# Second product of an MLP: order of emission on three engines, residual rows requested in three places, mixer weights in two rows

## Chip, cores and metric

The kernel runs on one core of one Trainium2 chip. The metric is the device time of one execution in microseconds, taken as the median of several runs.

## What is computed

A trunk of two layers over 1024 positions of width 1024, all in float32. Each layer has a token mixer (a gated MLP over chunks in the first layer, differential attention in the second), a squared-ReLU MLP of width 4096, and a per-layer gate:

```python
for i in range(DEPTH):
    a = _rmsnorm(h, g_mix_pre[i])
    m = _chunked_gmlp(a, ...) if i % N_MIXERS == 0 else _diff_attention(a, ...)
    h = h + _rmsnorm(m, g_mix_post[i])
    f = _sqrelu_mlp(_rmsnorm(h, g_ffn_pre[i]), f_w_up[i], f_w_down[i])
    h = h + _rmsnorm(f, g_ffn_post[i])
    gate = jax.nn.sigmoid(_rmsnorm(h, g_ple_pre[i]) @ ple_w_gate[i] + ple_b_gate[i])
    e = gate * (p[i] @ ple_w_proj[i])
    h = h + _rmsnorm(e, g_ple_post[i])

def _sqrelu_mlp(x, w_up, w_down):
    return jnp.square(jax.nn.relu(x @ w_up)) @ w_down
```

## The kernel before

Every operand of a product is cut into a high and a low part: ScalarE rounds it into `hi`, VectorE subtracts (`lo`), and TensorE makes three matmuls of 128x512 columns for each pair (`mm3`, L351 to L354). Both products of the MLP are done by a seven-product scheme on 2x2 blocks, so that sums and differences of blocks are formed on VectorE before and after.

**The second product** (in `ffn`, from L697). It has 56 steps `(g, c)`: groups g = 0, 1 and 2 have 16 steps each, group g = 3 has 8. A step is 24 matmuls: four places p, two halves e, three matmuls each. The text calls g = 0 to 3 the first to the fourth group. Around step m stand three jobs:

- `load_down(n)` requests the operands of step n on SP's queue: the activations `hid`, the weight blocks of `f_w_down`, and in the third and fourth group the stored sums `t4`. The operands go to one of seven rooms, the weights to buffers x from a ring (`sets`).
- `split_down(n)` forms the sums of weight blocks (L740 to L755) and cuts them (`cut`, L522 to L524). In the second and third group it also stores a sum to `t4`.
- `evict(g, p)` (L781 to L796) takes the banks of a place to the rows of `MA` when a group ends. TensorE cannot start the next group in a bank before it is evicted.

`after(t)`, called behind step t, emits the splits of step t + 2 or t + 3 (`lead_s`) and then the loads of step t + 7 (`lead_l`; fewer at the end).

The order of emission is not the order of execution. TensorE keeps it over the whole program (`manual_schedule` for PE); on the other engines a planner places the instructions at build time, by its own estimate of when each is ready, earlier emitted ones first among the ready ones.

**The rows behind it.** When the third group ends, `half` and `whole` finish rows of tiles 0 to 3 of the eight row tiles; those of 4 to 7 follow at the end of the fourth group. `whole` calls `residual` (L332), which takes the next of two buffers `hin`, requests the row tile of the residual stream (L336), adds (L340), stores it (L342), and lets `pre_norm` (L328 to L330) normalise it into a row of `MA`. `transpose_to` emits the eight transposes of each tile (L296) and their cuts (L282, L283) at a due time counted in matmul columns. The banks of the transposes are two, `PT`.

**Weights for the next stages** come through `WStream`: `load` requests a weight row into a buffer `raws` (L88) and cuts it into a slot (L119, L120). In the fourth group `ws.load()` is called for the gate's weights; `resident` loads four more operands, cut by ScalarE and GpSimd (L113, L114). `ple`, the gate, begins with a request of the bias row into `bbc` on GpSimd's queue (L847) and adds it at L862. `mixer1`, the second layer's mixer, takes its first weights through `[raw] + hin`.

Of the kernel before, what the change touches and what calls it, by code (L numbers as in the profile page):

```python
# [18 lines left out]
P = 128  # L19
D = 1024  # L20
T = 1024
NT = T // P
# [109 lines left out]
def _trunk(ctx, tc, nc, a, out):  # L132
# [197 lines left out]
        nc.scalar.activation(x, h, AF.Copy, scale=s)  # L330
        transpose_to(x, tt, us, gain)

    def residual(tt, t_ap, rs, hsrc, hdst, pre, gain=None):

        h = hinR.next()
        nc.sync.dma_start(h, hsrc[tt * P:(tt + 1) * P, :])  # L336
        w = D if pre or tt < NT - 1 else 512
        for c in range(0, D, w):
            cs = slice(c, c + w)
            nc.vector.scalar_tensor_tensor(out=h[:, cs], in0=t_ap[:, cs], scalar=rs, in1=h[:, cs],  # L340
                                           op0=ALU.mult, op1=ALU.add)
            nc.sync.dma_start(hdst[tt * P:(tt + 1) * P, cs], h[:, cs])  # L342
        if pre:
            pre_norm(h, tt, pre, gain)
# [170 lines left out]
    def ffn(i, hsrc, hdst, next_weights):  # L515
# [133 lines left out]
        def stream():  # L649
            for q in range(NQ):  # L650
                if q < 3:
                    settle((4, 6, 7)[q])
                yield from load_up(q)

        LEAD = 6
        loads = stream()
        early = [(q, n) for qs in ((0, 1), (2,), (3,), (4,)) for n in (1, 2) for q in qs]
        stage = [x.rearrange("p (r k f) -> p r k f", r=2, f=P) for x in (raw, bbc, raw, bbc, bbc)]
# [37 lines left out]
        def cols(x, k):  # L696
            return x[:, k * 512:k * 512 + 512]  # L697
# [1 line left out]
        sets = [  # L699
            Ring([(MA[:, 1], cols(MA[:, 2], 0)), (MA[:, 3], cols(MA[:, 2], 1)), (raw, cols(MA[:, 4], 0)),  # L700
                  (MA[:, 5], cols(MA[:, 4], 1)), (MA[:, 6], cols(bbc, 0))]),
            Ring([(x, cols(MA[:, t], 1)) for t, x in zip((0, 7, 2, 3, 4), hin + [xn[0], raw, bbc])]),
            Ring([(x, cols(MA[:, t], 1)) for t, x in zip((6, 5, 4, 7), [hin[1], raw, bbc, hin[0]])]),
        ]


        sumR = Ring([cols(xn[1], k) for k in range(2)])
        steps = [(g, c) for g in range(4) for c in range(NQ if g < 3 else NQ // 2)]
        loaded, cuts, ssq = {}, {}, {}

        def load_down(n):
            g, c = steps[n]
            room = last[c] if g == 3 else rooms[n % 7]
            hi, lo = [f32r(x.rearrange("p k t -> p (k t)")) for x in room]
            wh, hh, wl, hl = hi[:, 0:1024], hi[:, 1024:], lo[:, 0:1024], lo[:, 1024:]
            x = sets[g].next() if g < 3 else None
            if g == 3:
                for k in range(2):
                    nc.sync.dma_start(f32(cols(hl, k)), hid[2 * c + k][:, 3072:])
                nc.sync.dma_start(f32(wl), t4[c])  # L720
            else:
                if g == 2:
                    for k in range(2):
                        nc.sync.dma_start(cols(x[0], k), down[c, k, 1])
                    nc.sync.dma_start(x[1], cols(t4[c // 2], c % 2))
                else:
                    nc.sync.dma_start(x[0], down_rows[c, 0])
                    nc.sync.dma_start(x[1], down[c, 1, 1 - g])
                nc.sync.dma_start(f32(hl), hid[c][:, g * 1024:g * 1024 + 1024])
            loaded[n] = wh, wl, hh, hl, x  # L730

        def split_down(n):
            g, c = steps[n]
            wh, wl, hh, hl, x = loaded.pop(n)
            if g < 3:
                a1, a2 = cols(x[0], 0), cols(x[0], 1)
            if g == 0:

                t = sumR.next()
                vec(out=t, in0=a2, in1=a1, op=sub)  # L740
                vec(out=a2, in0=x[1], in1=t, op=sub)
                w = x[0],
            elif g == 1:

                t = sumR.next()
                vec(out=t, in0=a2, in1=a1, op=sub)
                vec(out=a1, in0=x[1], in1=a1, op=sub)
                nc.sync.dma_start(cols(t4[c // 2], c % 2), a1)
                w = x[1], t
            elif g == 2:  # L750

                t = sumR.next()
                vec(out=t, in0=a2, in1=a1, op=sub)
                vec(out=x[1], in0=x[1], in1=t, op=sub)
                nc.sync.dma_start(cols(t4[c // 2], c % 2), x[1])  # L755
                w = t, a2
            else:
                w = f32(wl),
            cut(hh, hl, f32(hl))
            k = D // len(w)  # L760
            for j, v in enumerate(w):
                cut(wh[:, j * k:j * k + k], wl[:, j * k:j * k + k], v)
            cuts[n] = wh, wl, hh, hl

        def after(t):

            for n in range(len(steps)):
                if n - t == lead_s[n]:
                    split_down(n)
            for n in range(len(steps)):  # L770
                if n - t == lead_l[n]:
                    load_down(n)

        for k, n in enumerate(rest_of):
            next(loads, None)
# [28 lines left out]
        def whole(tt, us):  # L804
            s = ssq[tt]
            vec(out=s[:, 0:1], in0=s[:, 0:1], in1=s[:, 1:2], op=add)
            rstd_of(s[:, 0:1], D, RMS_EPS)
            residual(tt, MA[:, tt, :], s[:, 0:1], hsrc, hdst, us)

        for m, (g, c) in enumerate(steps):  # L810
            wh, wl, hh, hl = cuts.pop(m)
            n_c = NQ if g < 3 else NQ // 2

            for p in range(4):
                for e in range(2):
                    bank = PM[p] if e == 0 or g == 3 else other[p]
                    cw = slice(e * 512, e * 512 + 512)
                    ch = slice(e * 512 + p * P, e * 512 + p * P + P)
                    mm3(bank, hh[:, ch], hl[:, ch], wh[:, cw], wl[:, cw],
                        c == 0 and (g < 3 or e == 0), c == n_c - 1 and (g < 3 or e == 1))  # L820
                if c == n_c - 1:
                    evict(g, p)
                    if g == 3:
                        half(p + 4, 0)
                        whole(p + 4, US_F + 4.0 * p)
            if g == 1 and c == 4:
                load_gbc(2 + i)
            if g == 2 and 2 <= c < 6:
                half(c - 2, 0)
            if c == n_c - 1 and g == 2:  # L830
                for p in range(4):
                    half(p, 1)
                    whole(p, US_F + 7 + 4.0 * p)
                for p in range(4):
                    half(p + 4, 1)
                next_weights(i)
            after(m)
            if g == 3:
                if c < 4:
                    ws.load()  # L840
                elif c < 6:
                    res[i] += [resident(i, 2 * c - 8), resident(i, 2 * c - 7)]
# [315 lines left out]
    def mixer1(gi, hsrc, hdst):  # L1158
# [3 lines left out]
        nc.gpsimd.dma_start(sgc, a["subln"])  # L1162
        nc.vector.tensor_scalar(out=sgc, in0=sgc, scalar1=1.0 - LAMBDA_INIT, scalar2=None, op0=ALU.mult)
        pbR.i = 2 * (pmR.i % 3)
        ws.raws = Ring([raw] + hin)
        for cb in range(2):
            qkv_qk(cb, qD, HD ** -0.5, cosT, sinT)
# [267 lines left out]
```

## Time and profile before

| | |
|---|---|
| time, median of 3 runs | 2401.24 us (2396.24 to 2403.47) |
| profiled execution | 2402.34 us, span 2400.6 us |
| TensorE matmul | 2327.9 us, 97%, 10748 instructions |
| VectorE | 1609.3 us, 67% |
| ScalarE | 1165.4 us, 49% |
| GpSimd | 228.0 us, 9% |
| granted TensorE clock, mean | 0.989 |

The span runs from the first to the last instruction of the profiled execution. A busy share is an average over stages with different limits, so stages are read by themselves. In the rows below PE is TensorE, PEld its weight loads, DVE VectorE, ACT ScalarE, POOL GpSimd and SP the queue that issues nearly all transfers; `out<-in` names the buffers, and what stands in brackets is idle time of the engine before the instruction and what ended it. L numbers are lines of the kernel before.

### The profile page before, as it was taken

Reading aid. Unit: us, or ns where it says so; the run is one execution under the profiler, and the core shown is the slowest. Engines: PE = TensorE matmul, PEld = TensorE weight load, DVE = VectorE, ACT = ScalarE, POOL = GpSimd, SP = SyncE. Lnnn points to the kernel's source line nnn. Section 1 sums busy time; section 2 is a strip of 40 time slices with the busy share of each in tenths; the row PEclk is TensorE's granted clock in tenths of the full one; section 3 lists DMA queues with packets and bytes.
Section 4 is the critical chain, followed back from the end, with each engine's and each line's share of the span. In section 5 each row is a group of like instructions: output and inputs, shape, how many; then the busy total and the mean of one; then the engine's idle time right before and its main releaser. Section 6 shows DMA issues by size and latency. Waiting matters only on the chain. (4 is left out here: it accounts for less than half of the span.)

```text
span 2400.6 us, 30544 instructions
## 1 busy us (share of the span) xinstructions
PE 2327.9 (97%) x10748; PEld 1924.2 (80%) x10748; DVE 1609.3 (67%) x2492; ACT 1165.4 (49%) x2003; POOL 228.0 (9%) x303
## 2 busy tenths in 40 slices
PE   9999999999999899999999989999999999989998
PEld 7888888888788687878887878777888888868787
DVE  4733697777866765563335888868877797675654
ACT  6232575555433355462224666657555554334551
POOL 1100100000000022010001342321000000000310
PEclk9999999999999999999999999999999999999999
DMA  9111545446977765244445765554544588777423
GB/s 330 57 35 54 165 142 202 145 156 223 355 249 236 250 233 183 74 169 142 147 154 179 218 181 143 158 184 137 189 159 164 173 335 279 243 256 245 176 106 123
DMA packets 200425, 441.03 MB, mean 184 GB/s; under 512 B 21040, under 2 KB 55856, under 8 KB 200144
## 3 DMA queue, kind: packets, MB, share of 16 engines
q1 hardware_dynamic: 199840, 437.89, 54.4%
q8 instruction: 85, 1.39, 0.2%
q0 software_dynamic: 432, 1.19, 0.2%
q14 instruction: 68, 0.56, 0.1%
HBM read 310.02 MB, written 133.17 MB: 185 GB/s over the span
## 5 line engine op out<-in xcount | busy, mean ns | idle before, releaser
L364 PE MATMUL pm_a<-w,xh 128*128 128x512 f32 x704 | 223.9, 396 | 1.3 <-ACT w L119 0.9
L364 PEld LDWEIGHTS pm_a<-w,xh 128*128 128x128 f32 x704 | 131.6, 189 | 29.8 <-ACT w L119 2.6
L523 ACT ACTIVATE xh<-xl 128x1024 fp32r<-128x1024 f32 x72 | 75.4, 1055 | 148.9 <-DMA xl<-hid 137.5
L364 PE MATMUL pb<-w,xh 128*128 128x512 f32 x416 | 134.9, 400 | 5.5 <-DVE gbc L972 2.9
L524 DVE TENSOR_TENSOR xl<-xl,xh 128x1024 fp32r<-128x1024 f32 x72 | 87.4, 1221 | 78.6 <-ACT xh L523 75.6
L364 PE MATMUL pm_a<-w,xl 128*128 128x512 f32 x352 | 138.7, 394 | 0.0
L523 ACT ACTIVATE w<-ma 128x512 fp32r<-128x512 f32 x130 | 82.2, 634 | 115.6 <-PE pm_a L353 39.5
L524 DVE TENSOR_TENSOR s<-s 128x1024 fp32r<-128x1024 f32 x56 | 68.0, 1222 | 58.9 <-ACT s L523 58.9
L523 ACT ACTIVATE s<-s 128x1024 fp32r<-128x1024 f32 x56 | 58.5, 1054 | 97.6 <-DMA s<-hid 80.6
L847 POOL DMA_DIRECT2D bbc<-in_ple_b_gate_dram x2 | 1.3, 628 | 1077.1 <-DVE s L524 1077.1
L353 PE MATMUL pm_a<-xl,w 128*128 128x512 f32 x260 | 101.4, 390 | 0.2 <-DVE xl L283 0.2
L352 PE MATMUL pm_a<-xh,w 128*128 128x512 f32 x260 | 101.6, 391 | 0.0
L354 PE MATMUL pm_a<-xh,w 128*128 128x512 f32 x260 | 101.2, 389 | 0.0
L364 PEld LDWEIGHTS pb<-w,xh 128*128 128x128 f32 x416 | 77.1, 190 | 20.1 <-DVE xn L394 3.4
L524 DVE TENSOR_TENSOR w<-ma,w 128x512 fp32r<-128x512 f32 x130 | 88.6, 683 | 0.7 <-ACT w L523 0.7
L243 POOL TENSOR_SCALAR small<-small 128x1 f32<-128x1 f32 x104 | 34.7, 333 | 553.9 <-DVE small L397 322.0
L340 DVE SCALAR_TENSOR_TENSOR hin<-ma,small,hin 128x1024 f32<-128x1024 f32 (+1 forms) x49 | 61.6, 1260 | 37.0 <-DMA hin<-h 24.5
L364 PE MATMUL pb<-w,xl 128*128 128x512 f32 x208 | 82.9, 399 | 0.0
L352 PE MATMUL pb<-xh,w 128*128 128x512 f32 x204 | 79.7, 391 | 0.0
L354 PE MATMUL pb<-xh,w 128*128 128x512 f32 x204 | 79.4, 389 | 0.0
L353 PE MATMUL pb<-xl,w 128*128 128x512 f32 x204 | 79.4, 389 | 0.0
L364 PEld LDWEIGHTS pm_a<-w,xl 128*128 128x128 f32 x352 | 66.4, 189 | 12.9
(476 smaller groups left out, 7048.2 us busy)
## 6 DMA issues: line engine op xcount, KB each, us to landing
xl<-hid SPq DMA_DIRECT2D x56, 512.0 KB, 5.1
ma<-in_f_w_up_dram SPq DMA_DIRECT2D x48, 512.0 KB, 3.7
h<-hin SPq DMA_DIRECT2D x40, 512.0 KB, 3.1
hid<-ma SPq DMA_DIRECT2D x80, 256.0 KB, 2.4
s<-hid SPq DMA_DIRECT2D x40, 512.0 KB, 5.2
hin<-h SPq DMA_DIRECT2D x40, 512.0 KB, 3.5
hid<-xn SPq DMA_DIRECT2D x64, 256.0 KB, 2.6
hid<-hin SPq DMA_DIRECT2D x64, 256.0 KB, 2.7
```

The lines of the kernel that those rows point to most:

```text
L243: nc.gpsimd.tensor_scalar(out=ss, in0=ss, scalar1=1.0 / n, scalar2=eps, op0=ALU.mult, op1=ALU.add)
L340: nc.vector.scalar_tensor_tensor(out=h[:, cs], in0=t_ap[:, cs], scalar=rs, in1=h[:, cs], op0=ALU.mult, op1=ALU.add)
L352: nc.tensor.matmul(ps, lhsT=lh, rhs=rh, start=start, stop=False)
L353: nc.tensor.matmul(ps, lhsT=lh, rhs=rl, start=False, stop=False)
L354: nc.tensor.matmul(ps, lhsT=ll, rhs=rh, start=False, stop=stop)
L364: nc.tensor.matmul(ps, lhsT=xs(l, kc, tt * P), rhs=r[:, cs], start=kc == 0 and k == 0, stop=kc == KC - 1 and k == 2)
L523: act(h, v, AF.Copy)
L524: vec(out=l, in0=v, in1=f32(h), op=sub)
L847: nc.gpsimd.dma_start(bbc, a["ple_b_gate"][i:i + 1, :].broadcast_to([P, D]))
```

## The change

- The steps of the first three groups up to step 44 (`FREE` = 45) are emitted inside a second `manual_schedule` that also covers SP, ScalarE and VectorE, so that these engines keep the order of emission there. `after` is rearranged: from step 9 on the loads come first, then the stores of `t4` collected from the split before, then the splits.
- The buffers of the second and third group are three rings of halves (`thirds`). The second group requests its weights as three pieces of 256 KB; the third takes `t4` into its own operand room.
- `residual` can be given its row. Rows are requested by `fetch` into `hin` and `bbc` in turn: 0 and 1 behind step 11 of the third group, 2 behind step 14, 3 to 6 at that group's end, and 7 in the fourth group's end.
- `mixer1` loads its next two weights through rows 2 and 3 of `MA` before it goes on with `[raw] + hin`.

```diff
--- before.py
+++ after.py
@@ -330,10 +330,14 @@
         nc.scalar.activation(x, h, AF.Copy, scale=s)
         transpose_to(x, tt, us, gain)
 
-    def residual(tt, t_ap, rs, hsrc, hdst, pre, gain=None):
-
-        h = hinR.next()
+    def load_h(h, tt, hsrc):
         nc.sync.dma_start(h, hsrc[tt * P:(tt + 1) * P, :])
+        return h
+
+    def residual(tt, t_ap, rs, hsrc, hdst, pre, gain=None, h=None):
+
+        if h is None:
+            h = load_h(hinR.next(), tt, hsrc)
         w = D if pre or tt < NT - 1 else 512
         for c in range(0, D, w):
             cs = slice(c, c + w)
@@ -653,6 +657,7 @@
                 yield from load_up(q)
 
         LEAD = 6
+        FREE = 3 * NQ - 3
         loads = stream()
         early = [(q, n) for qs in ((0, 1), (2,), (3,), (4,)) for n in (1, 2) for q in qs]
         stage = [x.rearrange("p (r k f) -> p r k f", r=2, f=P) for x in (raw, bbc, raw, bbc, bbc)]
@@ -699,21 +704,30 @@
         sets = [
             Ring([(MA[:, 1], cols(MA[:, 2], 0)), (MA[:, 3], cols(MA[:, 2], 1)), (raw, cols(MA[:, 4], 0)),
                   (MA[:, 5], cols(MA[:, 4], 1)), (MA[:, 6], cols(bbc, 0))]),
-            Ring([(x, cols(MA[:, t], 1)) for t, x in zip((0, 7, 2, 3, 4), hin + [xn[0], raw, bbc])]),
-            Ring([(x, cols(MA[:, t], 1)) for t, x in zip((6, 5, 4, 7), [hin[1], raw, bbc, hin[0]])]),
         ]
+
+
+        h0, h1, rw, bb, x0 = [[cols(x, k) for k in range(2)] for x in (*hin, raw, bbc, xn[0])]
+        ma = [cols(MA[:, t], 1) for t in range(NT)]
+        thirds = {
+            1: ([h0[0], h1[0], x0[0], rw[0], bb[0], ma[3], ma[2], ma[1]],
+                [x0[1], h0[1], h1[1], rw[1], ma[5]],
+                [ma[0], ma[7], bb[1], ma[4], ma[6]]),
+            2: ([ma[7], rw[0], h0[0], h1[0], bb[1], ma[4], bb[0]],
+                [h0[1], h1[1], rw[1], ma[5], ma[6]] * 3 + [x0[1]]),
+        }
 
 
         sumR = Ring([cols(xn[1], k) for k in range(2)])
         steps = [(g, c) for g in range(4) for c in range(NQ if g < 3 else NQ // 2)]
-        loaded, cuts, ssq = {}, {}, {}
+        loaded, cuts, ssq, stores = {}, {}, {}, []
 
         def load_down(n):
             g, c = steps[n]
             room = last[c] if g == 3 else rooms[n % 7]
             hi, lo = [f32r(x.rearrange("p k t -> p (k t)")) for x in room]
             wh, hh, wl, hl = hi[:, 0:1024], hi[:, 1024:], lo[:, 0:1024], lo[:, 1024:]
-            x = sets[g].next() if g < 3 else None
+            x = sets[0].next() if g == 0 else [r[c % len(r)] for r in thirds.get(g, ())]
             if g == 3:
                 for k in range(2):
                     nc.sync.dma_start(f32(cols(hl, k)), hid[2 * c + k][:, 3072:])
@@ -721,19 +735,24 @@
             else:
                 if g == 2:
                     for k in range(2):
-                        nc.sync.dma_start(cols(x[0], k), down[c, k, 1])
-                    nc.sync.dma_start(x[1], cols(t4[c // 2], c % 2))
+                        nc.sync.dma_start(x[k], down[c, k, 1])
+                elif g == 1:
+                    for k in range(2):
+                        nc.sync.dma_start(x[k], down[c, 0, k])
+                    nc.sync.dma_start(x[2], down[c, 1, 0])
                 else:
                     nc.sync.dma_start(x[0], down_rows[c, 0])
-                    nc.sync.dma_start(x[1], down[c, 1, 1 - g])
+                    nc.sync.dma_start(x[1], down[c, 1, 1])
                 nc.sync.dma_start(f32(hl), hid[c][:, g * 1024:g * 1024 + 1024])
+                if g == 2:
+                    nc.sync.dma_start(f32(cols(wl, 0)), cols(t4[c // 2], c % 2))
             loaded[n] = wh, wl, hh, hl, x
 
         def split_down(n):
             g, c = steps[n]
             wh, wl, hh, hl, x = loaded.pop(n)
             if g < 3:
-                a1, a2 = cols(x[0], 0), cols(x[0], 1)
+                a1, a2 = x[:2] if g else (cols(x[0], 0), cols(x[0], 1))
             if g == 0:
 
                 t = sumR.next()
@@ -744,15 +763,13 @@
 
                 t = sumR.next()
                 vec(out=t, in0=a2, in1=a1, op=sub)
-                vec(out=a1, in0=x[1], in1=a1, op=sub)
-                nc.sync.dma_start(cols(t4[c // 2], c % 2), a1)
-                w = x[1], t
+                vec(out=a1, in0=x[2], in1=a1, op=sub)
+                w = x[2], t
             elif g == 2:
 
                 t = sumR.next()
                 vec(out=t, in0=a2, in1=a1, op=sub)
-                vec(out=x[1], in0=x[1], in1=t, op=sub)
-                nc.sync.dma_start(cols(t4[c // 2], c % 2), x[1])
+                vec(out=a1, in0=f32(cols(wl, 0)), in1=t, op=sub)
                 w = t, a2
             else:
                 w = f32(wl),
@@ -760,16 +777,31 @@
             k = D // len(w)
             for j, v in enumerate(w):
                 cut(wh[:, j * k:j * k + k], wl[:, j * k:j * k + k], v)
+            if g in thirds:
+                stores.append((cols(t4[c // 2], c % 2), a1))
             cuts[n] = wh, wl, hh, hl
 
         def after(t):
 
+            def begin():
+                for n in range(len(steps)):
+                    if n - t == lead_l[n]:
+                        load_down(n)
+
+            def store():
+                while stores:
+                    nc.sync.dma_start(*stores.pop(0))
+
+            if t + 7 >= NQ:
+                begin()
+                store()
             for n in range(len(steps)):
                 if n - t == lead_s[n]:
                     split_down(n)
-            for n in range(len(steps)):
-                if n - t == lead_l[n]:
-                    load_down(n)
+            if t + 7 < NQ:
+                begin()
+            if t >= FREE:
+                store()
 
         for k, n in enumerate(rest_of):
             next(loads, None)
@@ -805,9 +837,23 @@
             s = ssq[tt]
             vec(out=s[:, 0:1], in0=s[:, 0:1], in1=s[:, 1:2], op=add)
             rstd_of(s[:, 0:1], D, RMS_EPS)
-            residual(tt, MA[:, tt, :], s[:, 0:1], hsrc, hdst, us)
-
+            residual(tt, MA[:, tt, :], s[:, 0:1], hsrc, hdst, us, h=rows.pop(tt))
+
+
+        rows, rowR = {}, Ring(hin + [bbc])
+
+        def fetch(*tts):
+            for tt in tts:
+                rows[tt] = load_h(rowR.next(), tt, hsrc)
+
+
+
+        E = mybir.EngineType
+        strict = tc.manual_schedule(engines={E.PE, E.SP, E.Activation, E.DVE})
+        strict.__enter__()
         for m, (g, c) in enumerate(steps):
+            if m == FREE:
+                strict.__exit__(None, None, None)
             wh, wl, hh, hl = cuts.pop(m)
             n_c = NQ if g < 3 else NQ // 2
 
@@ -823,6 +869,8 @@
                     if g == 3:
                         half(p + 4, 0)
                         whole(p + 4, US_F + 4.0 * p)
+                        if p == 0:
+                            fetch(7)
             if g == 1 and c == 4:
                 load_gbc(2 + i)
             if g == 2 and 2 <= c < 6:
@@ -831,10 +879,17 @@
                 for p in range(4):
                     half(p, 1)
                     whole(p, US_F + 7 + 4.0 * p)
+                    if p == 0:
+                        fetch(3)
+                fetch(4, 5, 6)
                 for p in range(4):
                     half(p + 4, 1)
                 next_weights(i)
             after(m)
+            if g == 2 and c == NQ - 5:
+                fetch(0, 1)
+            if g == 2 and c == NQ - 2:
+                fetch(2)
             if g == 3:
                 if c < 4:
                     ws.load()
@@ -1162,6 +1217,11 @@
         nc.gpsimd.dma_start(sgc, a["subln"])
         nc.vector.tensor_scalar(out=sgc, in0=sgc, scalar1=1.0 - LAMBDA_INIT, scalar2=None, op0=ALU.mult)
         pbR.i = 2 * (pmR.i % 3)
+
+        ws.raws = Ring([MA[:, 2, :], MA[:, 3, :]])
+        settle(3)
+        for _ in range(2):
+            ws.load()
         ws.raws = Ring([raw] + hin)
         for cb in range(2):
             qkv_qk(cb, qD, HD ** -0.5, cosT, sinT)
```

## The prediction

> **What bounds the kernel now.** I read the head of the page first, then the list of TensorE's waits, then the granted clock in short stretches, then the time lines around the longest waits.
>
> ```profile
> span 2400.6 us, 30544 instructions
> PE 2327.9 (97%) x10748; PEld 1924.2 (80%) x10748; DVE 1609.3 (67%) x2492; ACT 1165.4 (49%) x2003; POOL 228.0 (9%) x303
> ```
>
> TensorE is the bound, so only its idle time and its slow time can be won. All its idle time is 2400.6 - 2327.9 = 72.7 us. The list of waits says where the touched stages (second product, the rows behind it, the start of the mixer) hold some of it; columns are total us, times, longest.
>
> ```profile
> PE pt L296 <- DVE xl L283: 8.9, 3, 4.1
> PE pm_c L352 <- DVE ma L789: 8.3, 2, 8.1
> PE pm_a L352 <- DVE ma L789: 7.6, 1, 7.6
> PE pm_a L352 <- ACT s L119: 4.5, 1, 4.5
> ...
> PE pm_a L352 <- DVE hin L601: 2.3, 1, 2.3
> ...
> PE pm_a L352 <- DVE ma L794: 1.2, 1, 1.2
> PE pm_c L352 <- DVE ma L794: 1.2, 1, 1.2
> ...
> PE pt L352 <- DVE ma L787: 0.4, 1, 0.4
> ```
>
> A wait also costs after it ends. The stretches behind the waits (columns: window, length, busy time of each engine, then granted clock, DMA share, GB/s), with an undisturbed one first:
>
> ```profile
> 560.00:600.00 40.00, 40.00 (x179) 33.10 (x178) 31.96 (x48) 23.00 (x33) 0.00 (x0) 1.00 0.69 244
> 792.40:800.00 7.60, 7.45 (x18) 5.13 (x18) 7.60 (x13) 3.99 (x9) 0.00 (x0) 0.58 0.79 283
> 913.80:918.50 4.70, 4.70 (x18) 3.90 (x19) 1.92 (x3) 2.77 (x4) 3.56 (x2) 0.64 0.96 328
> 1065.00:1069.00 4.00, 4.00 (x11) 3.10 (x12) 1.38 (x2) 3.06 (x5) 0.74 (x2) 0.57 0.66 233
> 2135.00:2142.00 7.00, 6.63 (x17) 4.59 (x18) 7.00 (x11) 4.15 (x9) 0.00 (x0) 0.63 0.80 272
> 2256.30:2261.00 4.70, 4.63 (x18) 3.98 (x19) 2.00 (x4) 2.85 (x4) 3.62 (x2) 0.64 0.99 355
> ```
>
> Length times (1 - clock) is what each stall costs again: 7.60 x 0.42 = 3.2, 7.00 x 0.37 = 2.6, 4.70 x 0.36 = 1.7 twice, 4.00 x 0.43 = 1.7 us.
>
> **Part 1, order of emission on SP, ScalarE and VectorE (both layers).** The longest waits stand between the second and the third group. VectorE and ScalarE there, in the first layer:
>
> ```profile
> 788.80 1.06 ACT L523 ACTIVATE s<-s 128x1024 fp32r<-128x1024 f32 x1 [3.87 <-DMA s<-hid]
> 789.89 1.23 DVE L524 TENSOR_TENSOR s<-s 128x1024 fp32r<-128x1024 f32 x1 [2.21 <-ACT s L523]
> 791.63 0.68 DVE L789 TENSOR_TENSOR ma<-pm_a,ma 128x512 f32<-128x512 f32 x1
> 792.46 0.76 PE L352 MATMUL pm_a<-s 128*128 128x512 f32 x1 [7.57 <-DVE ma L789]
> ```
>
> L789 is the first eviction of the group; TensorE cannot start the next group before it. It stands on VectorE behind the cut of a step several steps ahead, and that cut waited for ScalarE, which waited for a transfer of hid. In the order of emission the evictions of the last step come before the cuts that are written after it, so L789 runs as soon as its bank is complete, three quarters of a step (4 us, below) before TensorE wants it. Its work is short (0.68 us), and what is late next is small: where the first and second group meet, the eviction (L787) is in time but for the 0.4 us at the foot of the list. Gain: 7.6 + 8.1 idle and 3.2 + 2.6 clock = 21.5 us.
>
> In the Trainium skill, "TensorE: Matmul & The Clock Gate", section "Part 1: The HAM clock gate", the clock halves after an idle window of about 3.4 us and returns after about 3.4 us of work. By that page one stall costs 1.7 us more, the two boundaries 3.4 instead of 5.8, and the sum would end 2.4 us higher; the trace, with stretches at 0.58 and 0.63 over 7 us and more, disagrees in the size, and I keep the rows.
>
> What the strict order can cost: an instruction that waits now holds all behind it on its engine for the 45 steps of groups one to three. Per step VectorE has two differences, one wide and two half cuts, 4 x 0.68 + 1.23 = 3.95 us, and TensorE 24 matmuls:
>
> ```profile
> 701.00:784.00 83.00, 83.00 (x366) 68.70 (x367) 52.34 (x71) 28.52 (x42) 0.00 (x0) 1.00 0.74 244
> 883.00:906.00 23.00, 21.75 (x101) 17.72 (x99) 19.50 (x26) 14.76 (x27) 13.77 (x15) 1.00 0.45 160
> ```
>
> 83.00 / 366 x 24 = 5.4 us. VectorE is 63% busy there, ScalarE 34%. Loads go out seven steps (38 us) and cuts three steps (16 us; two in the first group) ahead, and a load waits in SP's queue only for the end of a matmul step or a cut emitted before it. The stores of t4 now stand behind the next step's loads, at most one step later; their buffers come round after five to eight steps. I cover all that by the lead and cost it at nothing; without that cover each 0.1 us per step is 9 us over both layers. The new rings and the t4 row that lands in the step's own operand room move no bytes; the second group loads three times 256 KB where it loaded 512 and 256, one more issue per step, 32 in all, on a queue with room. Zero.
>
> The start of the second product waits on L601, 2.3 us: evictions of the first product. They are emitted outside the ordered stretch, so nothing new keeps cuts that are ready from going ahead of them. Between 2.3 us won and as much lost in each layer; I take 0, since the first two cuts and all of L601 stay outside.
>
> **Part 2, residual rows fetched in three places (both layers).** In the fourth group:
>
> ```profile
> 898.09 7.05 SPq L336 DMA_DIRECT2D hin<-h  x2
> 903.65 1.15 ACT L330 ACTIVATE ma<-hin,small 128x1024 f32<-128x1024 f32 x1 [1.42 <-POOL small L244]
> 909.12 1.29 DVE L340 SCALAR_TENSOR_TENSOR hin<-ma,small,hin 128x1024 f32<-128x1024 f32 x1 [5.31 <-DMA hin<-h]
> 910.44 1.06 ACT L328 ACTIVATE ma<-hin 128x1024 f32<-128x1024 f32 x1 [2.50 <-DVE hin L340]
> 912.44 1.06 ACT L282 ACTIVATE xh<-pt 128x512 fp32r<-128x512 f32 x2
> 913.79 0.66 PE L296 MATMUL pt<-identr,ma 128*128 128x128 f32 x4 [4.12 <-DVE xl L283]
> ```
>
> The two requests at 898.09 and just before 905.14 are the third and fourth row. The fourth waits for the second row's buffer, which L330 reads until 904.80. Its late landing stops L340, then ScalarE's L328, and behind that L282, which should have emptied the transposes' bank. With bbc as a third buffer the third row is there before the group ends and the fourth takes the first row's buffer, the one that the request at 898.09 got, 6.7 us before 904.80. L340 moves forward by about as much, L282 is next in line when its transposes end, and TensorE's wait goes. Late next is the transposes' own cut, 0.6 + 0.7 us, beside matmuls. Gain: 4.12 and its twin of 4.1 in the second layer, and twice 1.7 of clock: 11.7 us. Between 0 (ScalarE's order stays bad) and 11.7; I take 11.7, as the chain of six rows starts at the request that moves.
>
> bbc also takes the gate's bias row (L847, on GpSimd's queue), which now waits for the sixth row:
>
> ```profile
> DMA to landing us min/median/max: 5.4/5.6/5.7
> ...
> 947.02 1.14 ACT L330 ACTIVATE ma<-hin,small 128x1024 f32<-128x1024 f32 x1
> 961.13 0.71 PE L364 MATMUL pm_a<-w,xh 128*128 128x512 f32 x2
> ```
>
> The sixth row is read until 948.2; plus 5.6 the bias lands at 953.8. TensorE needs the first pair of banks back at 961.13 (fourth row tile), so 7 us are spare. Queued behind: GpSimd's roots of rows seven and eight, VectorE's later work behind L862. Cost 0; each us beyond the spare costs one, twice.
>
> **Part 3, gate weights pushed back, mixer weights in two rows.** The first four gate weights are cut today inside the third group (836 to 882 us, first layer):
>
> ```profile
> L120 DVE SCALAR_TENSOR_TENSOR w<-raw,gcol,w 128x512 fp32r<-128x512 f32 x8 | 5.7, 749 | 5.8 <-ACT w L119 5.8
> ```
>
> raw is in the ring until the group's last step now, so these eight (5.7 us of VectorE) fall into the stretch 883 to 906, where VectorE is 19.50 of 23 us busy. Bounds: 2.4 us won (the L794 waits) to 2 x 5.7 = 11.4 us lost. Cuts for the matmuls are emitted earlier than these and two of the residual rows no longer wait, so I stay near the low end: 1 us a layer, 2 us lost.
>
> The mixer, second layer only:
>
> ```profile
> 1059.87 0.33 SPq L88 DMA_DIRECT2D hin<-in_w_qkv_dram  x1
> 1064.21 1.33 ACT L119 ACTIVATE s<-hin,gcol 128x512 fp32r<-128x512 f32 x2 [1.28 <-DMA hin<-in_w_qkv_dram]
> ```
>
> The fourth weight goes out when a residual row lets hin go. In a row of MA, whose transposes the first product waits for anyway, it can go out before and land before 1060. Gain 4.5 (the fourth entry of the waits) + 1.7 = 6.2 us; at worst 0, as the buffer comes from rows that are read no more.
>
> **Sum.** The profiled execution took 2402.34 us (span 2400.6), 1.1 above the median 2401.24. 2402.3 - 21.5 - 11.7 - 6.2 + 2.0 = 2364.9, against the median 2363.8: **2364 us**.
>
> **Rivals.** *Only the boundaries come.* ScalarE's order between L328 and L282 is not fixed in the fourth group, which lies behind the ordered stretch, and the mixer's hoist is free too. Without both 2401.2 - 21.5 = 2379.7, with the mixer 2373.5: 2377 between them. *Crowding on VectorE.* The gate cuts land whole on the path, +9.4 over my 2: 2373. For it speaks this pair, where a sum of 128x1 takes 2.36 us beside GpSimd, longer than a cut of 128x1024 (1.23):
>
> ```profile
> 882.22 5.22 POOL L114 TENSOR_TENSOR s<-s 128x1024 fp32r<-128x1024 f32 x2 [33.16 <-ACT s L113]
> 885.09 2.36 DVE L806 TENSOR_TENSOR small<-small 128x1 f32<-128x1 f32 x1
> ```
>
> Four such holds a layer cost 2 x 4 x 2.36 = 18.9 us at most, 2383. The Trainium skill, "SBUF — State Buffer", section "Who interferes with whom", has that lock: a VectorE instruction with two SBUF inputs and a GpSimd one that reads block each other whole; the trace agrees with 2.36 us here. *The order does not bring the eviction forward*, or another wait stands there: 2401. *Slower:* one mechanism, head-of-line waiting in the strict stretch, a load on SP or a cut on VectorE that every step must sit out. It eats the gain at 37.4 / 90 = 0.42 us a step and shows as slower from 0.50; at 0.6 the time is 2364 + 54 = 2418. Against it stand 37% free VectorE and the leads above.
>
> **Numbers.** Forecast 0.49 (2354 to 2371), boundaries only 0.23, crowding 0.12, no effect 0.07, slower 0.09. The low end takes in the start of the product in both layers, L794 and no crowding (2364 - 4.6 - 2.4 - 2.0 = 2355, and up to 3 us, an estimate from the sizes above, for the clock behind the first of these); the high end boundaries only with part of the crowding, 2389. 0.3% is 7.2 us, about what can be told here: faster 0.84, same 0.07, slower 0.09.
>
> **What would show it.** Right: no L789 entry above 1 us among TensorE's waits; the clock at 1.00 behind the second group; L340 without a 5 us wait on hin, L283 gone as TensorE's releaser in the fourth group; L119 gone at the mixer's start; the first L862 later against the end of the fourth group by some 10 us. Wrong: TensorE waits on L524 in steps of groups one to three, new waits on L794 or L524 around 883, or on L862.

## Result and profile after

The changed kernel takes 2374.78 us (median of 4 runs, 2373.36 to 2375.9) where the kernel before takes 2402.35: a ratio of 0.9882, 95% interval 0.9869 to 0.9895. The forecast was 2364 us, the range 2352 to 2389. The median of before has one run more than in the table above. So the sign and the range held: 28 us came where 38 were forecast. The time lies above the forecast's own band (2354 to 2371) and next to the rival "only the boundaries come", which gave 2373.5 with the mixer's wait gone; and the parts differ more than the sum.

Line numbers from here on are those of the changed kernel: the eviction at the end of the second group is L821 (L789 before), that of the third L826 (L794), the residual's request L334, its addition L344, the first product's additions L605, the cuts of the second product L527 and L528.

The head of the page after:

```profile
span 2371.7 us, 30563 instructions
PE 2316.4 (98%) x10748; PEld 1919.4 (81%) x10748; DVE 1603.4 (68%) x2492; ACT 1167.3 (49%) x2003; POOL 235.7 (10%) x303
```

TensorE's idle time fell from 72.7 to 2371.7 - 2316.4 = 55.3 us, and its busy time by 11.5 us with the same 10748 matmuls, while the mean granted clock rose from 0.989 to 0.994. The list of TensorE's waits after (total us, times, longest), the rows of the touched stages:

```profile
PE pt L296 <- DVE xl L283: 7.3, 4, 3.9
PE pt L296 <- ACT ma L330: 4.4, 2, 2.2
...
PE pm_c L356 <- DVE ma L826: 3.9, 3, 1.9
...
PE pm_a L356 <- DVE ma L826: 2.2, 2, 1.6
...
PE pm_a L356 <- DVE hin L605: 0.6, 1, 0.6
```

L821 is not in the list, and neither is L119 on bank pm_a at the mixer's start; L283 is still there, L330 is new, and L826 has grown. Three stretches after, in the columns used above:

```profile
700.00:860.00 160.00, 160.00 (x708) 132.48 (x707) 121.15 (x164) 69.62 (x102) 0.00 (x0) 1.00 0.89 292
...
600.00:625.00 25.00, 24.28 (x106) 19.48 (x105) 24.89 (x31) 16.23 (x19) 0.00 (x0) 1.00 0.90 302
...
1040.00:1060.00 20.00, 20.00 (x99) 16.36 (x98) 12.90 (x22) 13.55 (x24) 2.83 (x7) 1.00 0.52 168
```

From the second to the end of the third group TensorE is busy 160.00 of 160 us at full clock: the boundary costs nothing. The start of the second product had 21.98 of 25 us and a clock of 0.93 before, by the row below. What went wrong stands behind the third group. Here are 65 us of each layer around the third group's end and the whole fourth group, first before (with the start of the product), then after:

```profile
880.00:945.00 65.00, 59.64 (x270) 48.70 (x270) 43.37 (x61) 37.55 (x63) 26.73 (x28) 0.97 0.46 164
2222.00:2287.00 65.00, 59.70 (x271) 48.96 (x270) 43.93 (x62) 36.96 (x62) 26.73 (x28) 0.97 0.46 168
600.00:625.00 25.00, 21.98 (x89) 17.38 (x88) 25.00 (x33) 14.73 (x18) 0.00 (x0) 0.93 1.02 387
```

```profile
861.50:926.50 65.00, 56.67 (x256) 45.83 (x255) 40.73 (x58) 37.05 (x61) 25.85 (x24) 0.97 0.51 184
2189.00:2254.00 65.00, 55.91 (x243) 44.49 (x242) 42.10 (x58) 36.52 (x62) 26.30 (x24) 0.95 0.47 172
```

TensorE gets through 270 and 271 matmuls in these 65 us before, and 256 and 243 after. At 0.227 us each (83.00 / 366, the prediction's row) that is 3.2 and 6.4 us given back.

There is a second way to count. TensorE runs its matmuls in the same order of buffers in all kernels of this document, so the nth matmul of one trace can be laid beside the nth of another, and the difference of their starts says how far ahead one kernel is, in the one profiled execution of each. The one that starts at 867.87 us after, just before the first of these waits, starts at 884.35 before: TensorE is 16.5 us ahead there. Behind the fourth group it is 13.1 us ahead, so 3.4 us are lost in the first layer; the second layer loses 6.4 by the same count.

The rows of the first layer, in order of time, show where:

```profile
867.28 0.75 DVE L120 SCALAR_TENSOR_TENSOR w<-raw,gcol,w 128x512 fp32r<-128x512 f32 x1
...
869.15 0.68 DVE L826 TENSOR_TENSOR ma<-pm_a,ma 128x512 f32<-128x512 f32 x1
...
881.66 1.05 ACT L328 ACTIVATE ma<-hin 128x1024 f32<-128x1024 f32 x1
...
884.30 3.21 POOL L244 TENSOR_TENSOR small<-small,mhalf 128x1 f32<-128x1 f32 x1
...
890.45 1.15 ACT L330 ACTIVATE ma<-hin,small 128x1024 f32<-128x1024 f32 x1 [7.65 <-POOL small L244]
891.62 0.32 SPq L334 DMA_DIRECT2D hin<-h  x1
891.65 0.66 PE L296 MATMUL pt<-identr,ma 128*128 128x128 f32 x4 [2.22 <-ACT ma L330]
892.04 0.38 SPq L515 DMA_DIRECT2D s<-p  x1
...
896.08 1.29 DVE L344 SCALAR_TENSOR_TENSOR hin<-ma,small,hin 128x1024 f32<-128x1024 f32 x1 [7.25 <-DMA hin<-h]
...
897.42 1.06 ACT L113 ACTIVATE s<-s 128x1024 fp32r<-128x1024 f32 x1 [2.69 <-DMA s<-p]
...
899.42 0.58 ACT L282 ACTIVATE xh<-pt 128x512 fp32r<-128x512 f32 x1
...
900.03 0.69 DVE L283 TENSOR_TENSOR xl<-pt,xh 128x512 fp32r<-128x512 f32 x1 [2.67 <-ACT xh L282]
...
900.78 1.12 PE L296 MATMUL pt<-identr,ma 128*128 128x128 f32 x4 [3.88 <-DVE xl L283]
```

The first row's square (L328) is done at 882.7, but its normalisation (L330) waits 7.65 us for GpSimd's root. GpSimd's queue has the roots of the later rows ahead of it, and they are stretched: one 128x1 operation takes 3.21 us. L330 ends at 891.60; at 891.62 SP can at last request the fourth row into the first row's buffer; VectorE waits 7.25 us for it, and TensorE 2.22 us for the first row.

TensorE's 3.88 us wait ends with the cut L283, and the path to it is not the one that the prediction followed before. L283 was ready on VectorE at 897.4, behind the fourth row, but it waited 2.67 us more for ScalarE's L282. ScalarE stood before it at L113, the split of a resident operand, 2.69 us for the transfer of that operand; and this transfer (s<-p, at 892.04) was requested on SP behind the fourth row's request, which had held SP's queue. The early requests only moved the buffer's owner: the fourth row waits for the first row now instead of the second, and the first row is late.

### The profile page after: what moved, and what is told of

The parts are those of the page before. It is cut to its first block, busy times and chain, and to the rows that moved or that the text cites. A ratio compares the mean times of both kernels' runs of the same rounds, so it can differ in the third digit from the quotient of the medians.

```text
span 2371.7 us, 30563 instructions
## 1 busy us (share of the span) xinstructions
PE 2316.4 (98%) x10748; PEld 1919.4 (81%) x10748; DVE 1603.4 (68%) x2492; ACT 1167.3 (49%) x2003; POOL 235.7 (10%) x303
## 4 chain that ended last, share of the span: by engine, by line
PE 64%; DVE 4%; DMA 3%; ACT 2%; POOL 1%; issue 1%; SPq 0%; DVEq 0%; POOLq 0%; ACTq 0%
PE pm_c L356 5%; PE pm_c L357 5%; PE pm_c L358 5%; PE pb L368 5%; PE pb L357 4%; PE pm_a L368 4%; PE pb L356 4%; PE pb L358 4%; PE pm_a L356 4%; PE pm_a L357 4%; PE pm_a L358 4%; PE pm_c L368 3%; PE pt L357 2%; PE pt L356 2%; PE pt L358 2%; DMA raw<-in_w_o_dram 1%
## 5 line engine op out<-in xcount | busy, mean ns | idle before, releaser
L527 ACT ACTIVATE w<-ma 128x512 fp32r<-128x512 f32 x130 | 82.3, 635 | 114.2 <-PE pm_a L357 40.4
L114 POOL TENSOR_TENSOR s<-s 128x1024 fp32r<-128x1024 f32 x8 | 19.8, 2486 | 1131.5 <-ACT s L113 570.3
L527 ACT ACTIVATE xh<-xl 128x1024 fp32r<-128x1024 f32 x72 | 75.2, 1053 | 80.4 <-DMA xl<-hid 71.4
L528 DVE TENSOR_TENSOR xl<-xl,xh 128x1024 fp32r<-128x1024 f32 x72 | 87.5, 1219 | 28.1 <-ACT xh L527 27.8
L243 POOL TENSOR_SCALAR small<-small 128x1 f32<-128x1 f32 x104 | 43.1, 414 | 530.1 <-DVE small L401 322.8
L528 DVE TENSOR_TENSOR w<-ma,w 128x512 fp32r<-128x512 f32 x130 | 88.5, 682 | 0.0
L527 ACT ACTIVATE s<-s 128x1024 fp32r<-128x1024 f32 x56 | 58.8, 1053 | 54.9 <-DMA s<-hid 38.2
L528 DVE TENSOR_TENSOR s<-s 128x1024 fp32r<-128x1024 f32 x56 | 68.1, 1220 | 22.0 <-ACT s L527 21.8
L344 DVE SCALAR_TENSOR_TENSOR hin<-ma,small,hin 128x1024 f32<-128x1024 f32 (+1 forms) x45 | 56.5, 1257 | 37.6 <-DMA hin<-h 22.8
L368 PEld LDWEIGHTS pm_a<-w,xl 128*128 128x128 f32 x352 | 66.2, 188 | 12.9
```

The costliest lines, as they stand in the source:

```text
L114: (eng or nc.vector).tensor_tensor(out=lo, in0=raw, in1=f32(hi), op=ALU.subtract)
L243: nc.gpsimd.tensor_scalar(out=ss, in0=ss, scalar1=1.0 / n, scalar2=eps, op0=ALU.mult, op1=ALU.add)
L368: nc.tensor.matmul(ps, lhsT=xs(l, kc, tt * P), rhs=r[:, cs], start=kc == 0 and k == 0, stop=kc == KC - 1 and k == 2)
L527: act(h, v, AF.Copy)
L528: vec(out=l, in0=v, in1=f32(h), op=sub)
```

## Experiments

Each kernel was compared with the kernel before on the same chip; the medians of before differ between chips (2400.97 to 2404.93), so the ratios are set side by side. A difference of 0.001 in the ratio is 2.4 us. Intervals are 95%.

**Order for TensorE alone**

```diff
-        strict = tc.manual_schedule(engines={E.PE, E.SP, E.Activation, E.DVE})
+        strict = tc.manual_schedule(engines={E.PE})
```

> The changed kernel with its ordered stretch kept for TensorE alone; rings, stores, rows and mixer weights stay changed. Theory: the order on the other engines took away the 7.57 and 8.10 us waits between the second and third group, so they come back in good part (L821 among TensorE's waits, 4 to 8 us a layer, the clock at half behind them), and with the wait at the start of the second product the time is 2385 to 2400 us. Rival: the deeper rings brought the operands earlier and took the waits away by themselves: 2375 us, no L821 above 1 us.

Ratio 0.9966 (0.9952 to 0.9981), 0.0084 or 20 us worse than the changed kernel. TensorE's waits:

```profile
PE pm_c L356 <- DVE ma L826: 7.4, 1, 7.4
PE pm_a L356 <- DVE ma L826: 7.2, 1, 7.2
...
PE pm_c L356 <- DVE ma L821: 4.2, 1, 4.2
...
PE pm_a L356 <- DVE ma L821: 3.9, 2, 3.6
...
PE pm_a L356 <- DVE hin L605: 2.4, 1, 2.4
```

The theory holds and the rival is half true: without the order L821 is back, but at 3.6 and 4.2 us, where the kernel before had 7.6 and 8.1. The rings, the t4 row in the operand room and the late stores, which stay in this kernel, account for the other half of the wait. In time they bring less: over this boundary the matmuls of this run gain 3.5 and 3.7 us on the kernel before, where those of the changed kernel gain 11.4 and 12.0. The order also keeps L826 and L605 short.

**Order for TensorE and VectorE**

```diff
-        strict = tc.manual_schedule(engines={E.PE, E.SP, E.Activation, E.DVE})
+        strict = tc.manual_schedule(engines={E.PE, E.DVE})
```

> The ordered stretch kept for TensorE and VectorE alone. Theory: only VectorE's order counts, since the eviction stood behind cuts on VectorE: 2372 to 2378 us, as the changed kernel (2374.8). Rival: a cut on VectorE still waits for ScalarE or for a transfer that these queues send late, and evictions behind it wait with it: 2380 to 2395 us, L821 back.

Ratio 0.9913 (0.9895 to 0.993), 0.0031 or 7 us worse, the intervals just touching. No wait on L821, and none above 0.8 us on L605: VectorE's order alone, with the new rings, does that. But at the third group's end:

```profile
PE pm_c L356 <- DVE ma L826: 9.3, 2, 8.6
PE pm_a L356 <- DVE ma L826: 9.2, 2, 8.6
```

VectorE's rows there, and what they waited for:

```profile
869.31 1.41 DVE L120 SCALAR_TENSOR_TENSOR w<-raw,gcol,w 128x512 fp32r<-128x512 f32 x2 [4.42 <-ACT w L119]
872.27 2.36 DVE L528 TENSOR_TENSOR xl<-xl,xh 128x1024 fp32r<-128x1024 f32 x2 [1.55 <-ACT xh L527]
...
875.15 0.68 DVE L826 TENSOR_TENSOR ma<-pm_a,ma 128x512 f32<-128x512 f32 x1
```

Neither theory foresaw the place. The ordered stretch ends at step 44; behind it the planner puts a gate weight's cut, still waiting for ScalarE, ahead of the evictions. That is the fault of the kernel before at another boundary.

**Rows requested where they are used**

```diff
-            residual(tt, MA[:, tt, :], s[:, 0:1], hsrc, hdst, us, h=rows.pop(tt))
+            residual(tt, MA[:, tt, :], s[:, 0:1], hsrc, hdst, us, h=rows.pop(tt, None))
...
-                rows[tt] = load_h(rowR.next(), tt, hsrc)
+                pass
```

> The changed kernel without the early requests: each residual row is requested where it is used, in the two buffers hin. Theory: the early rows bring nothing, because the fourth row waits for a buffer in either kernel (2.2 + 3.9 us of TensorE waits on the transposes in the fourth group now, 4.1 us before): 2372 to 2379 us. Rival: they bring the 11.7 us of the prediction, which something else hides: 2382 to 2388 us.

Ratio 0.9905 (0.9887 to 0.9923): 0.0023 or some 5 us worse, but the intervals overlap. Between the two expectations; the waits on L826 (4.0 and 3.9 us longest) and L283 (9.8 us in all) are longer than in the changed kernel. By the count of matmuls the end of the third group and the fourth group lose 9.2 and 8.2 us against before, where the changed kernel loses 3.4 and 6.4. So in this kernel the early rows bring some 5 us by the medians and 7.6 by the profiled executions, not 11.7; the intervals alone would allow anything from about zero to 11.

**Mixer's weights as before**

```diff
-        ws.raws = Ring([MA[:, 2, :], MA[:, 3, :]])
-        settle(3)
-        for _ in range(2):
-            ws.load()
```

> The changed kernel with the mixer's weights through raw and hin alone, as before. Theory: the two rows of MA took away the 4.48 us wait on L119 and 1.7 us of clock at the mixer's start, so the time is 6 us longer, 2381 us, and the wait is back. Rival: with all the work before it shifted the weights come in time through hin too: 2375 us.

Ratio 0.9903 (0.9886 to 0.992), 0.0021 or 5 us worse, the intervals overlapping. The profile decides: the wait is back, alone between 1030 and 1075 us, where the changed kernel has 0.3 us.

```profile
PE pm_a L356 <- ACT s L119: 5.6, 1, 5.6
```

**Four row buffers, first mapping**

```diff
-        rows, rowR = {}, Ring(hin + [bbc])
+        rows, rowR = {}, Ring([hin[0], hin[1], bbc, xn[1], bbc, hin[0], hin[1], hin[0]])
```

> The changed kernel with a fourth buffer for residual rows: rows 0 to 7 go to hin0, hin1, bbc, xn1, bbc, hin0, hin1, hin0, so that the fourth row no longer waits for the first row's buffer. Theory of the buffer: VectorE's 7.25 us wait on that row goes, with it TensorE's 3.9 us (first layer) and 2.8 us (second) on L283 and 1.7 us of clock each; the 2.2 us wait on L330 stays: 2365 to 2369 us. Rival, theory of the roots: the row is early but ScalarE and GpSimd are late all the same, the waits stay within 1 us: 2373 to 2377 us.

In this mapping the eighth row is requested into the sixth row's buffer before the sixth is used, so one row tile of the residual stream is replaced. Ratio 0.9846 (0.9825 to 0.9868), near what the buffer's theory said. It was repeated with another mapping:

```diff
-        rows, rowR = {}, Ring(hin + [bbc])
+        rows, rowR = {}, Ring([hin[0], hin[1], bbc, xn[1], hin[0], bbc, hin[1], hin[0]])
```

> The fourth row buffer with every row kept until it is used: rows 0 to 7 in hin0, hin1, bbc, xn1, hin0, bbc, hin1, hin0, the work whole. Theory of the buffer: as in the run with the first mapping, ratio to the kernel before 0.983 to 0.987, 2360 to 2369 us, no wait above 1 us on L283 in the middle of the fourth group, the 2.2 us wait on L330 still there. Rival: that run owed its gain to the eighth row that came too early: ratio 0.987 to 0.990, 2371 to 2377 us.

Ratio 0.9847 (0.9834 to 0.9861), 0.0035 or 8 us better than the changed kernel, the intervals apart. TensorE's waits in the first layer's fourth group:

```profile
PE pm_a L356 <- DVE ma L826: 3.3, 1, 3.3
PE pt L296 <- DVE xl L283: 1.9, 2, 1.4
PE pt L296 <- ACT ma L330: 1.1, 1, 1.1
```

The 3.9 us wait on L283 is gone. L330 stays (4.2 us in both layers), and L826 has grown by one microsecond in this layer. By the count of matmuls the first layer is 1.9 us better than the changed kernel and the second 6.7, and there L826 fell too, from 3.9 to 0.5 us. So the gain is shown, but not that the fourth row alone makes it: with the new buffer the planner also changed the order, and the first cut L282 now stands ahead of the L113 that held it.

```profile
896.81 0.58 ACT L282 ACTIVATE xh<-pt 128x512 fp32r<-128x512 f32 x1
897.71 1.06 ACT L113 ACTIVATE s<-s 128x1024 fp32r<-128x1024 f32 x1 [0.32 <-DMA s<-p]
```

**Roots left out, and roots with one GpSimd operation**

```diff
+        if root_on[0] is nc.vector:
+            nc.vector.tensor_scalar(out=ss, in0=ss, scalar1=0.0, scalar2=1.0, op0=ALU.mult, op1=ALU.add)
+            return
...
+                root_on[0] = nc.vector
...
+        root_on[0] = nc.gpsimd
```

> The changed kernel with the roots of the rows behind the second product left out (a constant 1 is written by VectorE in their place, so the rows are not normalised there); GpSimd keeps its two cuts of the resident operands. Theory of the roots: the first row's normalisation waited 7.65 us for GpSimd, whose small operations stand stretched (1.3 to 3.2 us each) beside VectorE, and the first row's buffer, the fourth row and both TensorE waits in the fourth group hang on that: all of them go, 2.2 + 3.9 + 1.7 and 2.2 + 2.8 + 1.7 us, 2358 to 2363 us. Rival, theory of the buffer or of VectorE's load: the waits move by less than 1.5 us each, 2370 to 2376 us.

Ratio 0.9864 (0.9843 to 0.9884). The wait on L330 went from 2.2 to 0.4 us in the first layer, but L283 kept 3.3 and 2.9 us, and L826 grew to 3.4 us in the first layer, which as a whole gained nothing (4.7 us lost against before, 3.4 in the changed kernel). The theory of the roots holds for the first wait alone; that the second wait hangs on the same root is wrong. The version with the work whole:

```diff
-            act(xn[0][:, 0:512], m, AF.Square, accum_out=ssq[tt][:, cb:cb + 1])
+            act(xn[0][:, 0:512], m, AF.Square, scale=1 / 32, accum_out=ssq[tt][:, cb:cb + 1])
...
-            vec(out=s[:, 0:1], in0=s[:, 0:1], in1=s[:, 1:2], op=add)
-            rstd_of(s[:, 0:1], D, RMS_EPS)
+            nc.vector.scalar_tensor_tensor(out=s[:, 0:1], in0=s[:, 0:1], scalar=RMS_EPS, in1=s[:, 1:2], op0=add, op1=add)
+            nc.gpsimd.tensor_tensor(out=s[:, 0:1], in0=s[:, 0:1], in1=mhalf[:, :1], op=ALU.pow)
```

> The changed kernel, its work whole, with one GpSimd operation instead of two for the first root of each row behind the second product: the square is scaled by 1/32 on ScalarE, the small constant joins VectorE's sum, and GpSimd only takes the power. Theory of the roots: 8 of 32 operations on that queue are gone in each layer, four of them ahead of the first row's normalisation, so that it comes 3 to 5 us earlier; the wait on L330 (2.2 us a layer) goes and the one on L283 shrinks: 2364 to 2370 us. Rival: GpSimd is held by VectorE whatever the number of its operations: 2373 to 2377 us.

Ratio 0.9865 (0.9847 to 0.9884), 0.0017 better, intervals overlapping: unclear. The wait on L330 shrinks to 0.5 us in each layer, and L283 rises from 7.3 to 8.5 us in all. With four buffers, in the first and the second mapping:

> The fourth row buffer and the single GpSimd operation together, the work whole. If both theories hold in part the two waits of the fourth group go in both layers: 2359 to 2365 us. If only the buffer counts: as with the buffer alone. If neither: 2375 us.

> The right four buffers and the single GpSimd operation for the first roots, the work whole. Theory of the roots beside the buffer: the wait on L330 shrinks from 2.2 to 1 us or less in each layer, 2 to 4 us under the run with four buffers alone. Rival: with the row early the roots cost nothing more, the time is within 2 us of it.

Ratios 0.9844 (0.9824 to 0.9864; the first mapping replaces a row tile as above) and 0.9837 (0.9824 to 0.9851), within 0.001 of the buffers alone. In the second, L330 has 2.9 and 3.2 us again. With four buffers the single operation is worth nothing that can be told.

**Gate weights staged in xn0**

```diff
                 if c < 4:
+                    ws.raws = Ring([xn[0]])
                     ws.load()
...
+        ws.raws = Ring([raw])
```

> The changed kernel with the gate's first weights staged in xn0 in place of raw, so that they cannot be requested before the third group's last squares: their cuts move behind the evictions at the end of the third group. Theory of crowding: these cuts (L120) stand ahead of the evictions that TensorE waits for (L826, 2.2 us in the first layer, 4.0 in the second) and ahead of the first row; both waits on L826 shrink below 1.5 us a layer: 2368 to 2373 us. Rival: the evictions themselves and the cuts for the fourth group fill VectorE there: L826 stays, 2374 to 2377 us, or the gate waits for its weights (TensorE waits on L119 or L120 at its start): above 2377 us.

Ratio 0.9817 (0.9804 to 0.9831), 2361.47 us: 0.0065 or 16 us better than the changed kernel, more than expected, and the best of all. The same 65 us of both layers, and TensorE's waits in the first:

```profile
864.00:929.00 65.00, 61.95 (x290) 50.23 (x289) 50.30 (x71) 42.78 (x73) 30.52 (x32) 1.00 0.58 207
2190.00:2255.00 65.00, 61.48 (x290) 49.66 (x290) 46.11 (x66) 45.88 (x76) 28.01 (x35) 1.00 0.62 221
```

```profile
PE pm_a L356 <- DVE ma L826: 1.6, 1, 1.6
PE pt L296 <- DVE xl L283: 1.4, 2, 1.2
```

290 matmuls against 256 and 243. By the count of matmuls the end of the third group and the fourth group are now 3.5 and 2.5 us faster than before. But the theory of crowding on L826 explains the smaller part: L826 fell from 2.2 to 1.6 us in the first layer and from 3.9 to 1.4 in the second, and the rest came from L330, L283 and the clock (0.97 and 0.95 in the changed kernel, 1.00 here), on which the theory said nothing in numbers. ScalarE's operations on the first row show that:

```profile
876.68 1.06 ACT L328 ACTIVATE ma<-hin 128x1024 f32<-128x1024 f32 x1
...
881.85 1.16 ACT L330 ACTIVATE ma<-hin,small 128x1024 f32<-128x1024 f32 x1 [2.65 <-POOL small L244]
```

L328 comes 5 us earlier, ahead of several squares of other rows, and L330 waits 2.65 us for its root where it waited 7.65. This is where the row stood in the kernel before, counted from TensorE's progress:

```profile
896.92 1.15 ACT L330 ACTIVATE ma<-hin,small 128x1024 f32<-128x1024 f32 x1 [2.65 <-POOL small L244]
```

This row of before is 12.6 us behind the matmul at 884.35. In the changed kernel the same distance is 890.45 - 867.87 = 22.6 us; with the late weights, where that matmul starts at 868.97, it is 12.9. So in the changed kernel the early weights put the first row back by 10 us, and moving them restores it. All three versions together:

> Four buffers, single GpSimd operation and late gate weights together, the work whole. If all three theories hold the third and fourth groups lose 2 to 5 us in each layer where the changed kernel loses 11 and 14: 2354 to 2362 us. If the late weights only move the crowd into the fourth group: as with the first two alone, 2361 to 2368 us.

Ratio 0.982 (0.9806 to 0.9833), 2362.18 us: as the late weights alone. With the first row early, its buffer comes free in time, and neither a fourth buffer nor fewer GpSimd operations add anything that can be told.

## Why the prediction was right or wrong

The count of matmuls gives each stage of the profiled executions its part (2402.34 - 2373.36 = 29 us in all):

| stage, both layers | forecast, us | found, us |
|---|---|---|
| start of the second product | 0 | 3.9 + 1.8 won |
| first to second group | 0 | 0.7 won, first layer |
| second to third group | 21.5 won | 11.4 + 12.0 won |
| third group's end and fourth group | 11.7 - 2 = 9.7 won | 3.4 + 6.4 lost |
| start of the mixer | 6.2 won | 6.2 won |
| stages that the change leaves alone | 0 | 2.7 won |

The last row varies by some 3 us between the runs of this document and is not assigned. So the total is near the forecast partly by luck: the fourth group missed by 19.5 us, and some 11 us that nobody forecast made up for part of it.

- **Boundary of second and third group, 21.5 us: right.** L821 is gone in both layers and the clock there is 1.00. The runs add that the order and the new rings share it: rings without the order leave 3.6 and 4.2 us.
- **Cost of the strict order, zero: right.** 160.00 of 160 us busy, with the transfers' share up from 0.74 to 0.89 and VectorE at 76%. The rival of waiting at the head of the queues did not happen in the ordered stretch.
- **Start of the second product, zero: wrong.** L605 fell from 2.3 + 0.7 us in the first layer to 0.6, and the clock there rose from 0.93 to 1.00, 1.7 us in 25; the second layer's 1.5 us are gone. The entries of before that the prediction's list leaves out:

```profile
PE pm_c L352 <- DVE hin L601: 1.5, 1, 1.5
PE pm_a L352 <- DVE gbc L601: 0.7, 1, 0.7
```

By the count above 5.7 us came. The failed step was "nothing new keeps cuts that are ready from going ahead of them": with the order on VectorE alone L605 stays short too, and without it 2.4 us are back. Not all of the gain is the order's: without it the clock in this stretch is 1.00 all the same, and 1.7 of the first layer's 3.9 us stay.
- **Rows, 11.7 us: wrong, and with the next term the main miss.** The step that failed is "the fourth takes the first row's buffer, the one that the request at 898.09 got". I took the first row's time from the trace of before. After, that row came late and its buffer free at 891.60. TensorE is 16.5 us ahead there, so on the clock of before this is 908.1: 10 us later than 898.09, and later even than the second row's 904.80, for which the fourth row waited before. The wait of 5.31 us became 7.25. The waits on the transposes are 6.1 us in the first layer and 5.1 in the second, where 4.1 stood in each before. The prediction also left out that the split L113 and its transfer queue behind the fourth row's request. Three buffers were not enough with the gate weights where they stand; with the late weights they were.
- **Gate weights, 2 us lost: the sign right, the working and the size wrong.** I said that all eight cuts fall behind the third group because raw is in the ring to its last step. Six of them were still done by 862 us, because the splits run ahead of TensorE; the two at 867.28 and 869.75 stand among the evictions. L826 costs 2.2 and 3.9 us where L794 cost 1.2 twice: 3.7 us more, where 2 were forecast for the whole term. But moving all eight away was worth 16 us: 8 us of it are waits on the transposes (11.2 us in the two layers, 3.2 with the late weights), the rest L826 and the clock. The term priced the length of the cuts; the runs show the cost in the row that they hold back. The rival "crowding" (2373 to 2383) was nearer to this stage than the forecast, by another path.
- **Bias row behind the sixth row, zero: right.** The row's request waited and VectorE with it, but TensorE has no wait there. The sign that was named for it came: counted from TensorE's progress, the first addition stands 14 us later than before (944.8 where 943.8 less 13.1 is 930.7).

```profile
938.37 0.63 POOL L902 DMA_DIRECT2D bbc<-in_ple_b_gate_dram  x1 [4.22 <-issue]
...
944.81 0.69 DVE L917 TENSOR_TENSOR xn<-pm_a,bbc 128x512 f32<-128x512 f32 x1 [0.36 <-DMA bbc<-in_ple_b_gate_dram]
```

- **Mixer, 6.2 us: right.** The wait is gone and comes back, 5.6 us long, with the old buffers; the time says 5 us, with an interval that does not exclude zero, and by the count of matmuls this stage then loses 1.8 us against before.

What stays open: how the gate weights at the third group's end hold the first row back by 10 us, when the two cuts among the evictions take 0.75 and 1.14 us. Their removal changes what the planner has ready at that moment, and with it the order on VectorE, ScalarE and GpSimd; whether the first row would do as well with the early weights and this order alone was not tried.

## What to carry to other kernels

A gain in one stage can be given back in the next, and the total hides it: where TensorE keeps its order, lay the nth matmul of one trace beside the nth of the other, and read each stage's part from the difference. When a row is to be fetched earlier, follow its buffer back to the last reader of the row before, on every engine, in the new timing. Where a planner orders the engines, one low-priority item that is ready at the wrong moment can cost more than its own length.

## What was not expected of the hardware

GpSimd's operations on 128x1 elements, 0.19 and 0.55 us at one row, took 2.56 and 3.21 us (L244 at 884.30, above) 7 to 9 us later, in a stretch in which VectorE scales, cuts and adds without a pause. GpSimd's rows after, in order of time:

```profile
874.63 0.19 POOL L243 TENSOR_SCALAR small<-small 128x1 f32<-128x1 f32 x1 [1.49 <-DVE small L838]
874.90 0.55 POOL L244 TENSOR_TENSOR small<-small,mhalf 128x1 f32<-128x1 f32 x1
...
881.65 2.56 POOL L243 TENSOR_SCALAR small<-small 128x1 f32<-128x1 f32 x1
...
889.60 0.19 POOL L243 TENSOR_SCALAR small<-small 128x1 f32<-128x1 f32 x1
889.87 0.55 POOL L244 TENSOR_TENSOR small<-small,mhalf 128x1 f32<-128x1 f32 x1
```

From 888.8 to 896.1 VectorE is idle, and there the same two operations take 0.19 and 0.55 us again. The prediction had the lock from the other side, as a hold on VectorE. The Trainium skill, "SBUF — State Buffer", section "Who interferes with whom", says that a VectorE instruction with two SBUF inputs contends with a GpSimd instruction that reads SBUF, and that the order of issue decides which of the two blocks, so a busy VectorE can hold GpSimd as well. The trace agrees in direction (3.21 us beside a busy VectorE, 0.55 beside an idle one); that the lock is the cause is read from it, not shown by a run of its own.
